# A hybrid decoder step on one core: an unsplit float32 pooling map, another order of the work up to attention, and a final norm that takes its Newton step on sums in PSUM

## The chip, the cores and the metric

The program runs on one core of a Trainium2 chip. The metric is the device time of one execution in microseconds (us). The kernel before is given by the median of three runs; one further execution was recorded by the hardware profiler, and its rows are what is quoted here.

A core has five engines that run side by side, each with its own queue of instructions, worked off in order: TensorE (PE in the profile, and PEld for its weight loads), VectorE (DVE), ScalarE (ACT), GpSimd (POOL) and SyncE (SP). An instruction that waits for another engine holds up everything behind it in its own queue. SP issues nearly all the DMAs here. POOL issues those that add what they read to what lies in SBUF.

## The reference, cut to what matters

One layer of a decoder for 1024 prompt tokens and 8 sample tokens, 1032 columns in all, width 1024:

```python
h = rmsnorm(x, g_mix); u = h @ w_in           # 512 pooling, 512 value, 512 gate columns
glu = val * sigmoid(gate)
ya = pool_mixer(a)      # windows 2/4/8/16: window mean - token; per group of 128 channels @ w_map; (+ b) * scale
yb = conv_mixer(glu)    # causal depthwise conv over 31 taps, LayerNorm over channels, silu
x = x + concat(ya, yb) @ w_out
x = x + cross_attn(rmsnorm(x, g_attn), k, v)  # 4 heads, 256 memory tokens; k, v = rmsnorm(mem) @ w_k, w_v
x = x + (silu(h @ w_gate) * (h @ w_up)) @ w_down,  h = rmsnorm(x, g_ffn)
y = x * rsqrt(mean(x * x) + 1e-6) * g_final   # the final norm
```

New keys, values and the tails of the pooling and convolution inputs are outputs too.

## The kernel before, in words

**Layout.** Channels lie on the 128 partitions and tokens along the row. A row of 1032 tokens is cut into three chunks of 344 columns for TensorE. Matrix products are made at float32 accuracy from two float32r operands each: `split` writes a rounded copy (the high half, on ACT or POOL) and the rest (the low half, on DVE or POOL), and `step3` issues three passes, high by high, high by low, low by high. `split_by_dma` makes the low half differently: ACT or POOL writes the high half and its negative, and a DMA issued by POOL adds the weights from DRAM to the negative. `BY_DMA` and `NOT_BY_DMA` say which weight tiles go that way.

**The order of the work.** Nothing is issued while the code runs: each step is a task with the engines that may do it, an estimated cost, and the buffers it reads and writes. `Program.order` then goes through the open tasks as a list scheduler: each engine takes the task that can start first by the plan, and among tasks that could start within a small slack the one with the lowest priority number. The number is the place in the program (and not above that of a follower), plus a bias. `ORDER` is the sequence, written out by hand, in which the parts up to the end of attention enter the program. A buffer is taken from a fixed number of slots of its kind: 19 large ones in SBUF (`op`), 3 for raw weights (`raw`), 2 for split weights (`w`), 3 scratch (`scr`), and in PSUM 2 wide ones of three banks (`mm`) and 2 of one bank (`ms`). So the estimated costs and the slots set the order on every queue, in later stages too. The chip then waits for semaphores, not for the plan.

**The parts that `ORDER` names and the prediction uses.** `g`, `v`, `A`: gate, value and pooling columns of `w_in`. `n`, `m`: norm and split of the memory. `K`, `V`: keys and values (tiles `kps`, `vps`, then `vf`, `vv`). `C` (`conv_sums`) and `D` (`conv_parts`): the convolution, by half-length sums (tiles `cp`, `y`) and by taps accumulated in PSUM (tile `cacc`); `s`: its sample tokens. `W` (`windows`): window sums by doubling on POOL or DVE (tile `win`), then `mean` on DVE, and a `split` of the result into `dop`, one large slot for each of the four groups. `M` (`mixer_out`): the map, `step3` on `dop` into `pmap` (a wide PSUM slot), from there ACT writes `yf` with bias and scale, and `yf` is split into `opa`. `L` (`layer_norm`): sums over channels by TensorE (`mean_ps`, `rstd_ps`), then `rsqrt_rows`, silu, split into `opb`. `O` and `B`: the output projection, first its four `opa` rows for all eight column tiles (tile `oa`), then the four `opb` rows (`ob`). After that come `q`, `S`, `T`, `P` for the prompt's attention, and `a` to `e` for the samples', which read the caches by DMA.

**After attention.** The projection `po`; then the feed-forward part as Strassen-like products of half blocks (tile `pr`), 22 tiles of gate and up, and four chunks of down; its last part, `last_down`, runs over `LAST_SPANS`, 516, 258 and 258 columns, with the rows' sums of squares collected in `fin`.

**The final norm** uses `rsqrt_rows` as the other norms do: sums over channels by a matmul with a matrix of 1/1024; on DVE m = -4(sum + eps); on ACT Ln, Exp and Square to get y = 1/(2 sqrt(sum + eps)) and y squared; on DVE t = m y^2 and y (t + 3), one Newton step, which gives 1/sqrt(sum + eps). `final` multiplies by it, for two of the eight row tiles at a time, and each pair is then written out by a DMA. `last_down` has multiplied by the weight `g_final` before.

Of the kernel before, what the change touches and what calls it, by code (L numbers as in the profile page):

```python
# [8 lines left out]
F32 = mybir.dt.float32  # L9
F32R = mybir.dt.float32r  # L10
AF = mybir.ActivationFunctionType
# [32 lines left out]
)  # L44

NOT_BY_DMA = (0, 1, 2, 16, 18, 19, 22, 23, 26, 27, 35, 36, 53, 54)
BY_DMA = ("w_in", "w_k", "w_v", "pool_map", "w_out_a", "w_out_b", "w_dn", "w_dn2")
# [5 lines left out]
SLACK = {"Pool": 0.3, "ACT": 0.3, "DVE": 0.05, "PE": 0.15}  # L53

# [15 lines left out]
    AF.Sigmoid: "sigmoid", AF.Silu: "silu", AF.Ln: "natural_log_exp_and_others", AF.Exp: "natural_log_exp_and_others",  # L70
# [18 lines left out]
class Program:  # L89
# [4 lines left out]
    SIGNAL, SIGNAL_PE, SAME = 0.2, 0.29, {"DVE": 0.12, "ACT": 0.1}  # L94

    def __init__(self, capacity):
        self.capacity = capacity
        self.tasks, self.writer, self.readers, self.later = [], {}, {}, 0

    def add(self, engines, emit, r=(), w=(), lock=False, func=None, nbytes=0):  # L100
        t = Task()
        t.engines = engines
# [140 lines left out]
def hybrid_step_kernel(ctx: ExitStack, tc: tile.TileContext, io):  # L243
# [38 lines left out]

    def act(n, ps=False, ptrs=0):
        return (0.05 if ps else 0.093) + 0.000833 * n + 0.093 * ptrs

    fixed = {"DVE": 0.065}

    def dve(n):
        return fixed["DVE"] + 0.00105 * n

    def pool_tt(n):
        return 0.09 + 0.00216 * n
# [6 lines left out]
    eps_t = const.tile([P, 1], F32, name="eps_t")  # L299
    nhalf = const.tile([P, 1], F32, name="nhalf")  # L300
# [18 lines left out]
    nc.gpsimd.memset(eps_t, EPS)  # L319
    nc.scalar.activation(nhalf, eps_t, AF.Copy)  # L320
# [42 lines left out]
    def split_by_dma(dst, key, src, n, r, again, again_keys, pool_too=False):  # L363


        def scaled(e, p, src, factor):
            if e is nc.scalar:
                e.activation(dst(p), src, AF.Copy, scale=factor)
# [6 lines left out]
        add({"Pool": 1.04}, lambda e: e.dma_start(dst(1), again(), accum_op=ALU.add), [key(1)] + again_keys, [key(1)], nbytes=4 * P * n)  # L375
# [20 lines left out]
    for part in ORDER.split():  # L396
        if part[0] == "M" and ("pool_map", 0) not in seq:
            seq.append(("pool_map", 0))
        seq += blocks.get(part[0], lambda i: [])(int(part[1:]))
# [7 lines left out]
    def w_load():  # L407
# [4 lines left out]
        width = 512 if name == "pool_map" else 1024  # L412
        raw = buf(f"raw{i}", "raw", (P, 1024))
        dma(lambda: raw[:, :width], lambda: io[name][j][:, :width], 512 * width, w=[(raw,)])
        raws[i] = (raw, width)
        state["loaded"] += 1

    def w_prep():
        i = state["prepped"]
        raw, width = raws.pop(i)  # L420
        name, j = seq[i]
        w = buf(f"w{i}", "op" if name in WIDE or i >= len(seq) - 4 else "w", (P, 2, 1024), F32R)
        if name in BY_DMA and i not in NOT_BY_DMA:
            split_by_dma(lambda p: w[:, p, :width], lambda p: (w, p), lambda: raw[:, :width], width, [(raw,)],
                         lambda: io[name][j][:, :width], [], name not in ("w_dn", "w_dn2"))
        else:
            split(lambda p: w[:, p, :width], lambda p: (w, p), lambda: raw[:, :width], width, [(raw,)])
# [23 lines left out]
    def step3(ps, w, wkeys, cols, x, k, first, last, spans=range(NCH), keys=None):  # L451
# [8 lines left out]
        add({"PE": 0.146 * 3 * len(spans)}, emit, list(wkeys) + (keys or [(x, 0), (x, 1)]),  # L460
# [12 lines left out]
    def rsqrt_rows(name, dst, dkeys, total, tkeys, ones, lo, width, at=None, more=None):  # L473
# [11 lines left out]
        for o, n in parts:  # L485
            ps = ms_buf(f"{name}_ps{o}")
            add({"PE": 0.1 + 0.0017 * n}, lambda e, ps=ps, o=o, n=n: e.matmul(
                ps[:, :n], ones, total[:, lo + o : lo + o + n], start=True, stop=more is None), tkeys, [(ps,)])
            if more is not None:
                add({"PE": 0.0017 * n}, lambda e, ps=ps, o=o, n=n: e.matmul(  # L490
                    ps[:, :n], ones, more[:, o : o + n], start=False, stop=True), [(more,)], [(ps,)])
# [16 lines left out]
    def small_products(e):  # L508
        e.tensor_tensor(pb_s, vec[:, V_PB : V_PB + 4], vec[:, V_PS : V_PS + 4], ALU.mult)
        taps = vec[:, V_CW : V_CW + 4 * CONV_K].rearrange("p (g k) -> p g k", g=4)[:, :, 1:].rearrange("p g (j two) -> p g j two", two=2)  # L510
        e.tensor_tensor(csum, taps[:, :, :, 0], taps[:, :, :, 1], ALU.add)

# [49 lines left out]
    add({"Pool": 0.5}, small_products, [("vec",)], [("small",)])  # L562
# [211 lines left out]
    a2 = [op_buf(f"a{i}") for i in range(2)]  # L774
    dops = {}

    def windows(g):
# [3 lines left out]
        tmp = op_buf(f"win{g}")  # L781
        add({"DVE": 0.07}, lambda e: e.tensor_copy(st_pool()[:, g, :, 15], ab[:, ai, SEQ:T]), [ak, (side, "pool")], [(side, "pool", g)])
# [24 lines left out]
        dops[g] = op_r(f"dop{g}")  # L807
        split(lambda p: dops[g][:, p], lambda p: (dops[g], p), cur, T, [ck])
# [11 lines left out]
    def keys(q):  # L820
        ps = mm_buf(f"kps{q}", 1)
        for i in range(2):
            w, wkeys = w_take("w_k")
            for k in range(KT):
# [4 lines left out]
                add({"PE": 0.327}, emit, wkeys + [(memg[k // 4], p, k % 4) for p in range(2)], [(ps,)])  # L829
# [62 lines left out]
    def values(c):  # L892
        ps = mm_buf(f"vps{c}", 2)
        for kk in range(4):
            w, wkeys = w_take("w_v")
            for k in (2 * kk, 2 * kk + 1):
# [6 lines left out]
                add({"PE": 1.3}, emit, wkeys + [(memg[k // 4], p, k % 4) for p in range(2)], [(ps,)])  # L903
# [76 lines left out]
    def scores(n):  # L980
# [23 lines left out]
        add({"PE": 1.31}, emit, [(qop[2 * h + dt], p) for dt in range(2) for p in range(2)] + [(kk, p, o) for p in range(2)], [pk])  # L1004
# [42 lines left out]
    def pv(n):  # L1047
# [4 lines left out]
        for c in range(2):  # L1052
# [8 lines left out]
            add({"PE": 1.3}, emit, [(v, 0), (v, 1)] + [(pT[h][m], p, c) for p in range(2) for m in range(2)], [(ps, c)])  # L1061
# [209 lines left out]
    def product(w, cols, xs, steps=1):  # L1271
# [21 lines left out]
        for n in range(0, nj, nj // steps):  # L1293
            js = range(n, n + nj // steps)
            add({"PE": 0.1195 * 6 * len(js)}, lambda e, js=js: emit(e, js),
# [230 lines left out]
    rsqrt_rows("Rf", Rf, RF, xss2, [(xss2,)], ones_d, 0, T)  # L1526
    for f in range(AHEAD):
        first_two(f)
    for f in range(FF_TILES):
# [5 lines left out]
        else:  # L1535
            fixed["DVE"] = 0.148
# [28 lines left out]

    last_w = {block: w_take(block[0]) for block in last_blocks}
# [3 lines left out]
    def last_down(c, n):  # L1570
# [19 lines left out]
        for w, keys, ks in ((wa, ka, range(4)), (wb, kb, (4, 5))):  # L1590
            add({"PE": 0.000425 * 3 * len(ks) * width}, lambda e, ks=ks: emit(e, ks),
# [8 lines left out]
        else:  # L1600
# [3 lines left out]
            e.activation(x2[j][:, i, sl], x2[j][:, i, sl], AF.Copy, scale=vcol(V_FIN, n)) if e is nc.scalar else  # L1604
            e.tensor_scalar(x2[j][:, i, sl], x2[j][:, i, sl], vcol(V_FIN, n), 1.0, ALU.mult, ALU.mult)), [xk], [xk])

    def final(c, j):
# [5 lines left out]
            [(fin, c)] + keys, keys, lock=True)  # L1613
# [126 lines left out]
```

## Time and profile before

| | |
|---|---|
| median of 3 runs | 1251.86 us (1251.17 to 1253.36) |
| profiled execution, its own time | 1254.77 us |
| its span | 1252.9 us |
| PE busy | 1215.9 us, 97% |
| DVE / ACT / POOL busy | 926.7 / 529.7 / 458.8 us |
| granted TensorE clock, mean | 0.99 |

The span is the time from the first to the last recorded event; 1.9 us of the execution's own time lie around it. A row of the timeline reads: start, duration, engine, line, operation, output and input tiles, shape, number of merged instructions, and in brackets the idle time of the engine before it with what ended that. A row of the stretches (the windows view) reads: stretch, its length, busy us and number of instructions of PE, PEld, DVE, ACT and POOL, granted TensorE clock (1.00 is full), busy share of the DMA engines, GB/s. A row of the groups (the lines view) reads: line, engine, operation, tiles, shapes, count, then busy us in all, mean ns of one, and the idle time before them.

### The profile page before, as it was taken

How to read it: one execution, taken by the hardware profiler on the slowest of the kernel's cores; microseconds unless marked ns; L12 is line 12 of the kernel's file. 1: busy time of each engine (PE TensorE's matmuls, PEld its weight loads, DVE VectorE, ACT ScalarE, POOL GpSimd, SP SyncE). 2: the span in 40 equal slices, each digit the busy share in tenths (PEclk: the TensorE clock that was granted, in tenths of full speed). 3: DMA queues.
4: the chain of work that ended last, by engine and by line, in shares of the span. 5: the costliest groups of instructions: out<-in, count | busy, mean ns of one | idle time of the engine just before them, and what ended most of it. 6: DMA issues, size and time to landing. Idle time of an engine off the chain costs nothing.

```text
span 1252.9 us, 22090 instructions
## 1 busy us (share of the span) xinstructions
PE 1215.9 (97%) x8958; PEld 1194.3 (95%) x8958; DVE 926.7 (74%) x1564; ACT 529.7 (42%) x731; POOL 458.8 (37%) x407
## 2 busy tenths in 40 slices
PE   8999996999999999999999999999999999999996
PEld 8999976999999879999999999999999999999996
DVE  7899988657367777679778677866867887778644
ACT  7766648454223453344322222222222364433644
POOL 3577841021101002113422233133324477778401
PEclk9999997999999999999999999999999999999998
DMA  7447686734255664231331332223322597778703
GB/s 281 104 84 169 142 241 177 213 88 163 104 194 207 238 225 169 102 132 38 112 126 60 111 110 102 104 67 111 106 85 89 205 312 198 206 181 206 175 26 111
DMA packets 59157, 183.86 MB, mean 147 GB/s; under 512 B 7920, under 2 KB 11696, under 8 KB 57776
## 3 DMA queue, kind: packets, MB, share of 16 engines
q1 hardware_dynamic: 52288, 157.74, 36.4%
q0 software_dynamic: 6768, 24.72, 11.2%
q8 instruction: 70, 1.15, 0.4%
q14 instruction: 31, 0.25, 0.1%
HBM read 148.80 MB, written 33.64 MB: 146 GB/s over the span
## 4 chain that ended last, share of the span: by engine, by line
PE 73%; DVE 10%; issue 7%; DMA 5%; ACT 2%; POOL 2%; SPq 0%; DVEq 0%; POOLq 0%; ACTq 0%
PE pr L1290 45%; PE ps L457 11%; PE fd L1587 6%; PE oa L457 4%; PE ob L457 4%; DVE cacc L663 2%; DMA raw<-in_w_v 2%; PE sc L1000 1%; DVE spcache_v L1097 1%; DMA spcache_k<-in_cache_k 1%; POOL w L357 1%; PE pv L1058 1%; DVE spcache_k L1097 1%; DMA w<-in_w_in 1%; DVE xss L384 1%
## 5 line engine op out<-in xcount | busy, mean ns | idle before, releaser
L1305 DVE TENSOR_TENSOR su<-pr,su 128x258 f32<-128x258 f32 (+1 forms) x204 | 109.3, 558 | 71.0 <-PE pr L1290 69.9
L1290 PE MATMUL pr<-ab,wTa 128*128 128x258 f32 x1056 | 134.2, 283 | 0.8 <-DVE su L1305 0.8
L1290 PE MATMUL pr<-ab,wG 128*128 128x258 f32 x1056 | 133.9, 283 | 0.8 <-ACT wU L346 0.8
L1290 PEld LDWEIGHTS pr<-ab,wTa 128*128 128x128 f32 x1056 | 130.1, 189 | 1.0 <-issue 1.0
L1290 PEld LDWEIGHTS pr<-ab,wG 128*128 128x128 f32 x1056 | 129.8, 189 | 1.2 <-ACT wU L346 1.1
L1290 PE MATMUL pr<-ab,wTb 128*128 128x258 f32 x1056 | 130.6, 283 | 0.0
L1290 PEld LDWEIGHTS pr<-ab,wTb 128*128 128x128 f32 x1056 | 128.6, 190 | 0.0
L457 PE MATMUL ps<-xop,w 128*128 128x344 f32 x720 | 114.1, 320 | 0.3 <-DMA w<-in_w_in 0.3
L457 PEld LDWEIGHTS ps<-xop,w 128*128 128x128 f32 x720 | 113.3, 188 | 0.6 <-DMA w<-in_w_in 0.6
L1290 PE MATMUL pr<-hb,dV 128*128 128x258 f32 x768 | 98.5, 284 | 1.1 <-ACT pp L1309 0.7
L1290 PEld LDWEIGHTS pr<-hb,dV 128*128 128x128 f32 x768 | 95.0, 189 | 1.8 <-ACT pp L1309 0.9
L457 PE MATMUL ps<-xq,w 128*128 128x344 f32 x576 | 94.8, 321 | 0.0
L457 PE MATMUL po<-oo,w 128*128 128x344 f32 x576 | 91.0, 320 | 0.4 <-DVE oo L1063 0.4
L457 PEld LDWEIGHTS po<-oo,w 128*128 128x128 f32 x576 | 90.7, 188 | 0.7 <-DVE oo L1063 0.7
L457 PEld LDWEIGHTS ps<-xq,w 128*128 128x128 f32 x576 | 90.6, 188 | 0.1
L1305 DVE TENSOR_TENSOR x<-pr,x 128x516 f32<-128x516 f32 (+1 forms) x122 | 63.3, 556 | 23.2 <-PE pr L1290 22.0
L663 DVE SCALAR_TENSOR_TENSOR cacc<-glu,vec,cacc 128x511 f32<-128x511 f32 (+14 forms) x116 | 77.0, 742 | 0.0
L1290 PE MATMUL pr<-hb,dW 128*128 128x258 f32 x576 | 75.0, 283 | 0.2 <-DVE x L1305 0.2
L1290 PEld LDWEIGHTS pr<-hb,dW 128*128 128x128 f32 x576 | 71.7, 189 | 0.4 <-DVE x L1305 0.4
L1587 PE MATMUL fd<-ho,w 128*128 128x258 f32 x576 | 70.0, 283 | 0.0
L346 ACT ACTIVATE w<-raw 128x1024 fp32r<-128x1024 f32 (+2 forms) x34 | 31.6, 932 | 90.2 <-issue 38.2
L1587 PEld LDWEIGHTS fd<-ho,w 128*128 128x128 f32 x576 | 69.5, 189 | 0.1
(323 smaller groups left out, 2338.5 us busy)
## 6 DMA issues: line engine op xcount, KB each, us to landing
gr<-in_w_gu SPq DMA_DIRECT2D x44, 512.0 KB, 3.4
hs<-hb SPq DMA_DIRECT2D x28, 516.0 KB, 4.2
hb<-su SPq DMA_DIRECT2D x8, 1032.0 KB, 4.9
dr<-in_w_dn SPq DMA_DIRECT2D x16, 512.0 KB, 6.2
hb<-hb POOLq DMA_DIRECT2D x12, 516.0 KB, 7.8
spcache_k<-in_cache_k SPq DMA_DIRECT2D x12, 512.0 KB, 5.0
raw<-in_w_in SPq DMA_DIRECT2D x10, 512.0 KB, 5.3
w<-in_w_in POOLq DMA_DIRECT2D x9, 512.0 KB, 6.6
```

The costliest lines, as they stand in the source:

```text
L346: e.activation(dst(0), src(), AF.Copy, scale=1.0 if gain is None else gain)
L357: e.tensor_tensor(dst(1), src(), f32(dst(0)), ALU.subtract)
L384: add({"Pool": pool_tt(n), "DVE": dve(n)}, lambda e: e.tensor_tensor(total(), total(), sq[:, i, :n], ALU.add), [(sq, i), tkey], [tkey], lo ...
L457: e.matmul(ps[:, c, :CW], w[:, wi, cols], x[:, xi, c * CW : (c + 1) * CW], start=first and p == 0, stop=last and p == 2)
L663: e.scalar_tensor_tensor(acc[h][:, n:], src[:, : HALF - n], w, acc[h][:, n:], ALU.mult, ALU.add)
L1000: e.matmul(bank()[:, i * NMEM : (i + 1) * NMEM], qop[2 * h + dt][:, qi, tt * P : (tt + 1) * P], kk[:, ki, 2 * (h % 2) + dt], start=(dt == ...
L1058: e.matmul(ps[:, c], v[:, vi, m, col : col + P], pT[h][m][:, pi, sl], start=(m == 0 and p == 0), stop=(m == 1 and p == 2))
L1097: e.scalar_tensor_tensor(piece[:, b], piece[:, b], 1.0, bc[:, b], ALU.mult, ALU.mult, accum_out=out(m)[:, first + b : first + b + 1])
L1290: e.matmul(bank(c), w[:, wi, cols(j)], xs[0](j, xi)[:, c * TQ : (c + 1) * TQ], start=j == 0 and p == 0, stop=j == nj - 1 and p == 2)
L1305: from_sums(sums, "DVE", dve, lambda e, src, sl: e.tensor_tensor(as_banks(o(sl), src), src, as_banks(a(sl), src), ALU.add), [akey], [okey])
L1587: e.matmul(view(i), w[:, wi, col : col + P], hops[k][:, xi, lo + i * width // count : lo + (i + 1) * width // count], start=(k == 0 and p ...
```

## The change

1. **The map.** The window results are no longer split, and `dop` is gone. `mixer_out` multiplies the raw map weights (`wmap`, one large slot, loaded when the first window part enters) with the float32 window result in one plain float32 matmul for each chunk. The map leaves the stream of split weights.
2. **The order.** A new `ORDER`, with other `LEAD`s (how far ahead a weight is prepared), a bias of 60 places on loads (0 before), and another choice of weights whose low half is made by DMA: `w_k` 1, 2, 3, 5, 7 (0 to 5 and 7 before); `w_v` 0, 1, 3, 5, 7 (0, 1, 5); `w_out_a` 0, 1, 3 (all four); `w_out_b` 2, 3 (0, 1); and now `w_q` 0, 3, 6 and `w_o` 4, 5, 6. For `w_in` and the last weights the choice stays.
3. **The planner's costs.** PE costs come from `pe(n)` and `pe32(n)`, with factors by stage in `MARGINS`; with these most costs of TensorE come out as before. A wait for TensorE's inputs is put at 0.35 us (0.29), a two-input operation on POOL at 0.05 us more, and the issue of an adding DMA on POOL at 0.6 us (1.04).
4. **The final norm.** `final_factors` takes the place of `rsqrt_rows`: ACT computes y = 1/sqrt(4 sum + 4 eps) from PSUM in one function, DVE computes (sum + eps) y from PSUM, times y, and (t - 0.75) y. The missing factor -4 is in the weights `gfin` = -4 `g_final`, made once at the start.

```diff
 ORDER = (
-    "A3 n0 g1 v1 C0 m0 g2 v2 m3 C1 m7 s0 m4 m6 g3 v3 m5 A2 A0 m1 s1 A1 m2 s2 K0 W3 K1 V1 V0 s3 W1 C2 W0 W2 K2 "
-    "M3 C3 D0 D1 M1 D2 M0 D3 K3 L0 M2 Y0 Z0 O0 O1 O2 O3 B0 B1 B2 B3 q0 q1 f0 S0 a0 b0 c0 q2 S2 q3 S4 a1 b1 S7 S6 c1 "
...
+    "m4 m7 A3 n0 g1 m0 v1 g2 v2 g3 m2 m3 m6 C0 m5 C1 m1 v3 A2 A0 s1 A1 s0 K0 s2 K1 W3 K2 V1 W0 W1 D0 s3 V0 M1 M0 "
+    "W2 C2 C3 D1 D2 M3 K3 Y0 D3 M2 L0 O0 O1 O2 O3 Z0 B0 B1 B2 B3 q0 q1 a0 f0 b0 c0 q2 q3 a1 b1 S4 S7 S0 S5 S6 c1 "
...
-LEAD = {"w_k": 4, "w_v": 3, "pool_map": 1, "w_out_a": 3, "w_q": 5, "w_in": 2, "w_out_b": 5, "w_o": 5}
+LEAD = {"w_k": 3, "w_v": 3, "w_out_a": 1, "w_q": 9, "w_in": 2, "w_out_b": 8, "w_o": 8}
-BIAS = {"evac": 10, "prep": 20, "load": 0}
+BIAS = {"evac": 10, "prep": 20, "load": 60}
...
-    SIGNAL, SIGNAL_PE, SAME = 0.2, 0.29, {"DVE": 0.12, "ACT": 0.1}
+    SIGNAL, SIGNAL_PE, SAME = 0.2, 0.35, {"DVE": 0.12, "ACT": 0.1}
...
     def windows(g):
...
+        if not dops:
+            dma(lambda: wmap[:], lambda: io["pool_map"][0], 512 * 512, w=[(wmap,)])
...
-        dops[g] = op_r(f"dop{g}")
-        split(lambda p: dops[g][:, p], lambda p: (dops[g], p), cur, T, [ck])
+        dops[g] = cur, ck
...
     def mixer_out(g):
-        if not opa:
-            state["wm"] = w_take("pool_map")
-        wmap, wmk = state["wm"]
         ps = mm_buf(f"pmap{g}")
-        step3(ps, wmap, wmk, block_cols(g), dops[g], 0, True, True)
+        cur, ck = dops[g]
+
+        def emit(e):
+            for c in range(NCH):
+                e.matmul(ps[:, c, :CW], wmap[:, block_cols(g)], cur()[:, c * CW : (c + 1) * CW], start=True, stop=True)
+
+        add({"PE": NCH * pe32(CW)}, emit, [(wmap,), ck], all3(ps))
...
+    def final_factors(c):
...
+            add({"ACT": act(n, True)}, lambda e, ps=ps, n=n, dl=dl: e.activation(
+                fin[:, dl], ps[:, :n], AF.Abs_reciprocal_sqrt, bias=eps4, scale=4.0), [(ps,), (fin, c)], [yk], func=AF.Abs_reciprocal_sqrt)
...
+            add({"DVE": dve(n)}, lambda e, ps=ps, n=n, sl=sl, dl=dl: e.scalar_tensor_tensor(
+                t[:, sl], ps[:, :n], EPS, fin[:, dl], ALU.add, ALU.mult), [(ps,), yk], [(t, sl.start)])
+            add({"DVE": dve(n)}, lambda e, sl=sl, dl=dl: e.tensor_tensor(t[:, sl], t[:, sl], fin[:, dl], ALU.mult),
+                [(t, sl.start), yk], [(t, sl.start)], lock=True)
+            add({"DVE": dve(n)}, lambda e, sl=sl, dl=dl: e.scalar_tensor_tensor(
+                fin[:, dl], t[:, sl], -0.75, fin[:, dl], ALU.add, ALU.mult), [(t, sl.start), yk], [yk], lock=True)
...
-        rsqrt_rows(f"fin{c}", fin, [(fin, c)], fin, [(fin, c)], ones_d, lo, width, more=last_sq.get(c))
+        fkeys = final_factors(c)
         for j in range(4):
-            final(c, j)
+            final(c, j, fkeys)
```

More of the change, by code (lines that the diff above doesn't have):

```diff
@@ L93 @@
     DMA_LATENCY, DMA_RATE, DMA_ISSUE, TABLE = 0.95, 0.36e6, 0.45, 1.28
-    SIGNAL, SIGNAL_PE, SAME = 0.2, 0.29, {"DVE": 0.12, "ACT": 0.1}
+    SIGNAL, SIGNAL_PE, SAME = 0.2, 0.35, {"DVE": 0.12, "ACT": 0.1}
     def __init__(self, capacity):
         self.capacity = capacity
-        self.tasks, self.writer, self.readers, self.later = [], {}, {}, 0
+        self.tasks, self.writer, self.readers, self.later, self.margin = [], {}, {}, 0, MARGINS["early"]
     def add(self, engines, emit, r=(), w=(), lock=False, func=None, nbytes=0):
         t = Task()
-        t.engines = engines
+        t.engines = {}
+        for e, cost in engines.items():
+            factor, more = self.margin.get(e, (1, 0)) if not nbytes else (1, 0)
+            t.engines[e] = cost * factor + more
         t.emit, t.lock, t.func, t.nbytes = emit, lock, func, nbytes
@@ L487, in rsqrt_rows @@
             add({"PE": 0.1 + 0.0017 * n}, lambda e, ps=ps, o=o, n=n: e.matmul(
[L488 to L491, printed above, removed]
+                ps[:, :n], ones, total[:, lo + o : lo + o + n], start=True, stop=True), tkeys, [(ps,)])
             add({"DVE": dve(n)}, lambda e, ps=ps, o=o, n=n: e.tensor_scalar(
@@ L1535, in hybrid_step_kernel @@
         else:
-            fixed["DVE"] = 0.148
+            pg.margin = MARGINS["down"]
             later(lambda: dn_load(0), "load")
@@ L1563, in hybrid_step_kernel @@
         hidden_load(f)
+    pg.margin = MARGINS["last"]
     last_w = {block: w_take(block[0]) for block in last_blocks}
```

87 lines of the change are left out of this document (57 added, 30 removed), and 4 rows, old and new, of the table ORDER.

## The prediction, made before the changed kernel was built or run

> **What bounds the kernel now.** I read the page's shares first, then the stretches of 20 us, then TensorE's own timeline where it is not full.
>
> ```profile
> PE 1215.9 (97%) x8958; PEld 1194.3 (95%) x8958; DVE 926.7 (74%) x1564; ACT 529.7 (42%) x731; POOL 458.8 (37%) x407
> ```
> ```profile
> 160.00:180.00 20.00, 20.00 (x91) 16.39 (x90) 16.14 (x26) 12.01 (x14) 7.08 (x8) 1.00 0.86 257
> 180.00:200.00 20.00, 10.77 (x70) 9.27 (x69) 19.11 (x26) 12.21 (x15) 6.00 (x7) 0.87 0.80 208
> 200.00:220.00 20.00, 16.76 (x90) 16.30 (x91) 16.61 (x20) 16.13 (x20) 3.26 (x3) 0.76 0.64 170
> 220.00:240.00 20.00, 20.00 (x116) 19.04 (x116) 15.03 (x24) 7.00 (x9) 1.94 (x2) 0.95 0.85 275
> ...
> 400.00:440.00 40.00, 37.72 (x253) 36.09 (x253) 30.02 (x106) 16.82 (x41) 3.06 (x10) 1.00 0.65 231
> 440.00:480.00 40.00, 37.46 (x215) 32.65 (x215) 34.01 (x132) 15.20 (x34) 3.88 (x12) 1.00 0.66 240
> ...
> 700.00:800.00 100.00, 100.00 (x834) 100.00 (x833) 74.05 (x107) 26.19 (x35) 32.72 (x21) 1.00 0.27 93
> ```
> TensorE is the bound: of the 1252.9 us span it is idle for 37. The stretch from 700 stands for the long middle: 834 matmuls in 100 us, no gap, so nothing to gain there. One place stands out, 180 to 220, with 12.5 us idle and the clock granted at 0.87 and 0.76. TensorE's timeline there:
>
> ```profile
> 99.79 15.74 PE L457 MATMUL ps<-xop,w 128*128 128x344 f32 x99
> ...
> 148.99 11.62 PE L827 MATMUL kps<-memg,w 128*128 128x256 f32 x96
> 160.44 22.27 PE L901 MATMUL vps<-w,memg 128*128 128x512 f32 x96
> 182.55 3.57 PE L827 MATMUL kps<-memg,w 128*128 128x256 f32 x26
> 187.98 2.86 PE L827 MATMUL kps<-memg,w 128*128 128x256 f32 x22 [1.86 <-DMA w<-in_w_k]
> 193.22 1.83 PE L457 MATMUL pmap<-dop,w 128*128 128x344 f32 x9 [2.37 <-ACT vf L906]
> 199.95 5.31 PE L457 MATMUL pmap<-dop,w 128*128 128x344 f32 x18 [4.91 <-ACT yf L848]
> ...
> 208.79 1.21 PE L457 MATMUL pmap<-dop,w 128*128 128x344 f32 x6 [0.22 <-DVE dop L357]
> ...
> 215.84 15.80 PE L457 MATMUL oa<-opa,w 128*128 128x344 f32 x81 [3.02 <-ACT yf L848]
> ```
> A 344-wide matmul takes 0.159 us when all is well (15.74/99), a 256-wide one 0.121 (11.62/96). From 182.55 to 215.84 TensorE did the last 96 `kps` and all 36 `pmap` matmuls, 11.6 + 5.7 = 17.3 us of work in 33.3 us: 16.0 lost. The five waits in brackets are 12.4 of it. The other 3.6 is clock: after the wait of 4.91 us, 18 matmuls worth 2.9 took 5.31. The first 81 `oa`, worth 12.9, took 15.8, another 2.9. So 18.9 us hang on this place.
>
> The Trainium skill, "TensorE: Matmul & The Clock Gate", Part 1, says that the array's clock is halved after an idle window of about 3.4 us and comes back only after as long a busy one. The trace agrees with it: of the waits above only the one of 4.91 us is longer than that, and the 18 matmuls right behind it run at half speed.
>
> Why TensorE starves there is read on the other engines:
>
> ```profile
> 172.89 7.86 DVE L663 SCALAR_TENSOR_TENSOR cacc<-glu,vec,cacc 128x504 f32<-128x504 f32 x12
> 176.61 0.86 POOL L375 DMA_DIRECT2D w<-in_w_k  x1 [10.58 <-ACT w L368]
> 185.75 0.68 DVE L357 TENSOR_TENSOR w<-raw,w 128x512 fp32r<-128x512 f32 x1
> 187.96 1.07 ACT L346 ACTIVATE dop<-win 128x1032 fp32r<-128x1032 f32 x1 [6.84 <-DVE win L804]
> 191.91 1.25 ACT L906 ACTIVATE vf<-vps,rmc 128x512 f32<-128x512 f32 x2
> ```
> DVE spends 7.9 us on taps while windows are still to do (`dop` waits for one until 187.96), and POOL, which may do window sums, idles 10.6. ACT then stands 6.84 us with `dop`'s high half at its head, and behind it is `vf`, which has to empty `vps`: ready at 182.7 (160.44 + 22.27), done from 191.91 on. `vps` holds one of two wide PSUM slots, and `pmap` at 193.22 had waited for `vf`.
>
> **The change, part by part.** *The map.* Four splits and one weight split go:
>
> ```profile
> L357 DVE TENSOR_TENSOR dop<-win,dop 128x1032 fp32r<-128x1032 f32 x4 | 4.9, 1230 | 2.8 <-ACT dop L346 2.8
> L346 ACT ACTIVATE dop<-win 128x1032 fp32r<-128x1032 f32 x4 | 4.2, 1055 | 6.8 <-DVE win L804 6.8
> L868 PE MATMUL mean_ps<-ysum,ones_c 128*128 128x512 f32 x4 | 1.9, 592 | 0.0
> ```
> DVE loses 4.9 + 0.7 (the weight's low half at 185.75) = 5.6 us, ACT 4.2 and its stand. Each window comes 1.06 + 1.23 = 2.3 us closer to its map. Four large slots fall away and one is added. In return TensorE multiplies in plain float32. The nearest row is `mean_ps`: two 512-wide matmuls give four records in 1.9 us, so 0.95 each, 0.64 at 344 columns; three a map, four maps: 7.7 us against 5.7, so +2.0. If cost did not fall with width it would be 12 x 0.95 = 11.4, +5.7; if the passes saved paid for all, 0. I take +2.0, as the 344- and 256-wide rows above go by width. The map's load stays one SP DMA, moved ahead of K and V loads and out of the three raw slots.
>
> *The order.* `W3 W0 W1` now stand before `V0`, `M1 M0` right behind it, ahead of `C2 C3 D1 D2 D3`; so windows may take the DVE time that taps took at 172.89, and taps move under `O`, where DVE had 5 us idle in 220 to 240 alone. If all 18.9 us go, `O` ends 18.9 - 2.0 = 16.9 earlier. But `O` covers the LayerNorm, which needs all of the convolution:
>
> ```profile
> 222.66 1.06 POOL L646 TENSOR_TENSOR y<-y,cp 128x497 f32<-128x497 f32 x1 [7.58 <-DVE y L646]
> ...
> 263.89 2.51 DVE L357 TENSOR_TENSOR opb<-y,opb 128x1032 fp32r<-128x1032 f32 x2
> 268.22 7.09 PE L457 MATMUL ob<-opb,w 128*128 128x344 f32 x44
> ```
> The convolution's last tap is at 222.66, the first `opb` is ready at 263.89 + 1.25 = 265.1, and `ob` starts at 268.22 because `O` ends there: 3.1 us of cover. So `ob` can start earlier only as far as the LayerNorm does. At worst for a gain that is 265.1 (-3.1); with DVE's 5.6 us it is 259.5 (-8.7); with `O` alone as the limit 251.3 (-16.9). I take -8.7, the one that rests on removed work and not on idle time refilled; `opb` is late next.
>
> *Weights.* `w_k` 0 and 4 and `w_out_a` 2 gain a low half on DVE or POOL, `w_v` 3 and 7 lose one: +1, at 1.23 us on DVE, and POOL's idle 10.6 us covers it; without that cover +1.2. Six `w_q` and `w_o` tiles lose theirs, and get an ACT pass (1.06) and a POOL issue (0.86) each; in 400 to 480 ACT is busy 32 of 80 us and POOL 7, so nothing, at most the six issues, +5.2, and -4.8 (both gaps of TensorE there, 2.3 + 2.5) if DVE, 64 of 80, was what it waited for. The samples' parts of `ORDER` move in the same stretch, with the same two ends. I take 0.
>
> *Planner's costs and the bias on loads.* They can reshuffle every later queue. TensorE has no gap from 600 to 1000 to close, so this can only lose. What hides it are raw weights loaded ahead:
>
> ```profile
> gr<-in_w_gu SPq DMA_DIRECT2D x44, 512.0 KB, 3.4
> ```
> One late load costs up to its 3.4 us. I take 0: loads start when one of three raw slots comes free, whatever the bias.
>
> *The final norm.* Behind the last matmul:
>
> ```profile
> 1242.85 0.70 PE L490 MATMUL fin_ps<-fsq,ones_d 128*128 128x258 f32 x2 [0.59 <-ACT fsq L1602]
> 1243.59 0.43 DVE L492 TENSOR_SCALAR fin_m<-fin_ps 128x258 f32<-128x258 f32 x1 [1.30 <-PE fin_ps L490]
> 1244.05 0.42 ACT L499 ACTIVATE fin_t<-fin_m 128x258 f32<-128x258 f32 x1 [0.71 <-DVE fin_m L492]
> ...
> 1246.33 2.52 DVE L1611 TENSOR_TENSOR x<-x,fin 128x516 f32<-128x516 f32 x4
> ```
> From 1243.59 to 1246.33 stand six steps (DVE, ACT three times, DVE twice), 0.457 each with the hop. Four remain (ACT, DVE three times): 2 x 0.457 = -0.9. The new function needs its table once, as Ln and Exp did:
>
> ```profile
> 1209.43 1.28 ACT L1636 ACT_TABLE_LOAD   x1
> ```
> It lies 33 us before the end, under `fd` matmuls. If Square were not in the new set, each change back would put 1.28 on the last span: +0.4 in sum. The first span's sums stay longer in two one-bank slots that `fd` needs too; at most one table load of waiting, +1.3. I take -0.9.
>
> Sum: -8.7 + 0 + 0 + 0 - 0.9 = -9.6 on the span of 1252.9, so 1243.3; the profiled execution took 1254.77, 2.9 above the median of 1251.86, so the median goes to 1242.3.
>
> **The rivals.**
> *Everything is recovered.* DVE's idle time fills too, and `O` is the limit: -16.9 - 0.9, so 1234. For it: POOL's long idle; against: the 42 us from the convolution's last tap to the first `opb`, which no part of the change shortens.
> *The LayerNorm stays where it is.* `ob` starts at 265.1: -3.1 - 0.9, so 1248.
> *One long wait stays.* By the two readings of the stall: if a wait as long as the 4.91 one remains, half of the 12.4 stays, and the slow clock behind it with 6.5: only -6.2 + 2.0 - 0.9, so 1247. By the rule in the Trainium skill, "TensorE: Matmul & The Clock Gate", Part 1, the slow clock is a step: a wait cut from 4.91 to 3.5 saves none of it. By a slope it would go by half too, and the sum would be 1244.
> *It doesn't do what it says.* The windows stay late for want of slots, behind K and V weights in the same large slots; -0.9 and +2.0: 1253.
> *Slower: the convolution comes last.* The windows' own work on DVE:
>
> ```profile
> L804 DVE SCALAR_TENSOR_TENSOR win<-win,a 128x1032 f32<-128x1032 f32 x4 | 4.9, 1234 | 0.1
> L791 DVE TENSOR_TENSOR win<-win 128x1022 f32<-128x1022 f32 x3 | 3.6, 1216 | 0.0
> ```
>  `C2 C3` now stand behind all windows and `V0`. If `C3`'s chain of taps, which ends at 222.66, starts later by the windows put in front (four groups, 2.4 us of last sum and mean each, so about 9), `opb` is ready at 274 and `ob` starts 6 us late: +6 - 0.9, so 1257. It decides from 4 us of delay on (3.1 of cover and 0.9 at the end). For it: 15 dependent taps in each chain; against: 5.6 us less on DVE, and an idle POOL.
>
> **How the numbers follow.** The forecast has 0.42 (1236 to 1246 by itself), everything 0.10, LayerNorm fixed 0.11, a long wait 0.12, no effect 0.09, slower 0.16. About 0.2%, 2.5 us, is what a measurement of this kernel can tell from no change. Faster is the first four, 0.75; no effect is 0.09; slower 0.16. The range goes from 1231, full recovery with most of the 4.8 us at 400 to 480 on top, to 1257.
>
> **What would show it.** Right: no `dop`; `pmap` with 24 records, about 7.7 us; TensorE's idle time in 180 to 220 under 5 us and its clock back at 1.00; `ob` starting at 255 to 262, waiting for `opb` just before; 0.9 us less between the last `fin_ps` and the first `final`. Wrong: gaps of several us in 200 to 260 behind `opb`, a granted clock under 0.9 there, waits for DMA in 320 to 480, fewer than 834 matmuls per 100 us in the middle, or a second table load after 1215.

## The result, and the profile after

The changed kernel took 1253.16 us (median of 14 runs, 1249.64 to 1259.84); the kernel before took 1251.96 us on the same chips (14 runs, 1251.17 to 1253.7). The ratio is 1.001, with a 95% interval of 1.000 to 1.0021: at most 0.2% slower and not faster. The forecast was 1242.3.

The change did most of what the sum said, and then lost it again. This table puts the two profiled executions beside each other (the changed kernel's took 1253.93 us, its span is 1252.2). Each line gives the start of a stage's first matmul on TensorE, in us.

| stage | before | after | difference |
|---|---|---|---|
| output projection, first half (`oa`) | 215.84 | 210.59 | -5.25 |
| output projection, second half (`ob`) | 268.22 | 260.33 | -7.89 |
| gate and up (`pr<-ab`) | 558.04 | 549.30 | -8.74 |
| down (`pr<-hb`) | 1006.27 | 1001.26 | -5.01 |
| last part (`fd`) | 1170.89 | 1171.11 | +0.22 |
| end of the last `fin_ps` | 1243.55 | 1243.73 | +0.18 |
| end of the span | 1252.9 | 1252.2 | -0.7 |

Up to the gate the kernel is 8.7 us ahead. The gate and up stage gives 3.7 back and the down stage 5.2. The tail behind the last `fin_ps` gains 0.9.

The early part first. TensorE's timeline of the changed kernel, to be held against that of before in the prediction:

```profile
166.72 16.82 PE L918 MATMUL vps<-w,memg 128*128 128x512 f32 x72
188.68 3.78 PE L861 MATMUL pmap<-win,wmap 128*128 128x344 f32 x6 [5.14 <-DVE win L819]
...
197.94 3.63 PE L861 MATMUL pmap<-win,wmap 128*128 128x344 f32 x12
...
207.31 1.90 PE L861 MATMUL pmap<-win,wmap 128*128 128x344 f32 x6
210.59 8.79 PE L471 MATMUL oa<-opa,w 128*128 128x344 f32 x54 [1.38 <-DVE kf L845]
...
260.33 9.90 PE L471 MATMUL ob<-opb,w 128*128 128x344 f32 x62
```

And the stretches of the same kernel (length, then busy us and count of PE, PEld, DVE, ACT and POOL, the granted clock, DMA share, GB/s):

```profile
180.00:200.00 20.00, 14.86 (x54) 10.74 (x53) 17.03 (x26) 11.47 (x13) 8.65 (x7) 0.83 0.63 174
200.00:220.00 20.00, 18.54 (x116) 16.35 (x115) 15.89 (x20) 11.48 (x14) 2.26 (x3) 1.00 0.86 234
...
600.00:1000.00 400.00, 400.00 (x3328) 400.00 (x3327) 296.89 (x423) 106.53 (x141) 127.89 (x81) 1.00 0.30 107
1000.00:1170.00 170.00, 163.96 (x1346) 162.52 (x1345) 136.02 (x216) 76.53 (x97) 130.29 (x114) 1.00 0.78 213
```

Between 180 and 220 TensorE is now idle for 6.6 us; it was 12.5. One long wait is left, 5.14 us for the window of the first map, and the clock is down behind it: six `pmap` records (two for each float32 matmul) take 3.78 us, where the last six take 1.90. Behind that all goes well, and `oa` runs at the full clock from its start. It covers the way to `ob` in 49.7 us (52.4 before), and this is 2.6 of the 7.9 us.

The middle is as full as before: 3328 matmuls in 400 us. The down stage isn't. The same stretches of the kernel before:

```profile
600.00:1000.00 400.00, 400.00 (x3330) 400.00 (x3329) 299.85 (x427) 106.58 (x143) 128.32 (x82) 1.00 0.30 104
1000.00:1170.00 170.00, 168.64 (x1391) 167.74 (x1390) 132.77 (x222) 78.78 (x98) 130.15 (x111) 1.00 0.81 221
```

From 1000 to 1170 TensorE was idle for 1.4 us, and now it is for 6.0. What it waits for from 540 to 1245 is read in the waits view (engine, what waited and for what; us in all, times, longest), first of the kernel before:

```profile
PE pr L1290 <- ACT wU L346: 0.8, 1, 0.8
PE pr L1290 <- DVE su L1305: 0.8, 1, 0.8
PE pr L1290 <- ACT pp L1309: 0.7, 1, 0.7
PE pr L1290 <- DVE x L1305: 0.6, 2, 0.4
...
```

and then of the changed one:

```profile
PE pr L1307 <- DVE x L1322: 4.0, 4, 1.8
PE pr L1307 <- ACT wG L363: 1.3, 1, 1.3
PE pr L1307 <- DVE wG L374: 1.0, 1, 1.0
PE pr L1307 <- DVE su L1322: 0.9, 1, 0.9
...
PE fd L1606 <- DVE x L1322: 0.8, 1, 0.8
...
```

`x` and `su` on DVE are the sums that empty the PSUM slots of `pr`, and `wG` is the second gate tile's weight, whose split on ACT and DVE comes late, not its load. No DMA is in the list. The tail is as forecast. ACT reads PSUM itself and DVE takes three steps:

```profile
1243.77 0.48 ACT L1642 ACTIVATE fin<-fin_ps,eps 128x258 f32<-128x258 f32 x1 [0.25 <-PE fin_ps L1640]
1244.28 0.43 DVE L1646 SCALAR_TENSOR_TENSOR fin_t<-fin_ps,fin 128x258 f32<-128x258 f32 x1 [1.81 <-ACT fin L1642]
...
1245.67 2.51 DVE L1658 TENSOR_TENSOR x<-x,fin 128x516 f32<-128x516 f32 x4
```

From 1243.77 to 1245.67 there are 1.90 us; the six steps took 2.74.

### The profile page after: what moved, and what is told of

Its sections match the earlier page's. It is cut to its first block, busy times and chain, and to the rows that moved or that the text cites. A ratio compares the mean times of both kernels' runs of the same rounds, so it can differ in the third digit from the quotient of the medians.

```text
span 1252.2 us, 22041 instructions
## 1 busy us (share of the span) xinstructions
PE 1217.0 (97%) x8946; PEld 1191.6 (95%) x8946; DVE 928.5 (74%) x1548; ACT 516.3 (41%) x715; POOL 481.8 (38%) x428
## 4 chain that ended last, share of the span: by engine, by line
PE 49%; DVE 3%; DMA 1%; issue 1%; POOL 0%; ACT 0%; DVEq 0%; SPq 0%; ACTq 0%; POOLq 0%
PE pr L1307 44%; PE fd L1606 6%; DMA dr<-in_w_dn 1%; DVE hb L374 1%; DVE x L1322 1%; DMA hs<-hb 0%; DVE dW L374 0%; POOL dt L1448 0%; DVE su L1348 0%; DVE dV L374 0%; DVE pp L1330 0%; DVE x L1658 0%; DVE pp L1322 0%; DVE dt L1448 0%; PE fin_ps L1637 0%
## 5 line engine op out<-in xcount | busy, mean ns | idle before, releaser
L1307 PE MATMUL pr<-ab,wU 128*128 128x258 f32 x528 | 67.4, 284 | 0.0
```

What stands on the lines that cost most here:

```text
L1307: e.matmul(bank(c), w[:, wi, cols(j)], xs[0](j, xi)[:, c * TQ : (c + 1) * TQ], start=j == 0 and p == 0, stop=j == nj - 1 and p == 2)
```

## The experiments

Nothing in the change touches the code of the feed-forward part. Only the planner's costs reach it, through the order on the queues. That makes the first theory: **the late costs give the early gain back.** Its rival is that a kernel that comes to the gate earlier, in another state, loses the time whatever the costs. The planner has one set of constants, so the runs change them at one point of the program, where the feed-forward part begins. Ratios are to the kernel before, on the same chip.

**e1: the old costs from the feed-forward part on.**

```diff
     pg.margin = MARGINS["gated"]
+    pg.SIGNAL_PE = 0.29
+    late["pool"] = 0.09        # pool_tt(n) returns late["pool"] + 0.00216 * n
+    issue["dma"] = 1.04        # cost of issuing an adding DMA on POOL
+    # and the bias on loads is 0 again
```

> The changed kernel, but from the feed-forward part on the planner uses the costs of before again (0.29 for TensorE's wait, 0.09 on POOL, 1.04 for an adding DMA's issue, no bias on loads). Theory A, the 7.9 us won up to `ob` and the 0.9 at the end are real and the new planner costs give the rest back by reordering the down stage: faster than before by 6 to 8.5 us, 1244 to 1246, and no wait of TensorE over 1 us between 1000 and 1180 - about 8. Theory B, the feed-forward part loses because it starts 8 us earlier, before its weights and DVE are ready, whatever the costs: no faster than the changed kernel, 1252 to 1254.

1248.52 us, ratio 0.9958 (0.9942 to 0.9973), so 5.3 us faster than before and 6.5 faster than the changed kernel by the two ratios. That is short of the 6 to 8.5 that the theory asked for. The down stage takes 165.0 us (before 164.6, changed 169.9). The rival, by which nothing would be gained over the changed kernel, falls: the same early part goes before it.

**e2: the opposite, the kernel before with the new costs from the feed-forward part on.** The same four constants, the other way round.

> The kernel before, with the new planner costs from the feed-forward part on and nothing else. Theory A: slower than before by 4 to 7 us, 1256 to 1259, with the waits for DVE behind `x` in the down stage that the changed kernel shows. Theory B: the same as before within 1 us, 1251 to 1253.

1268.22 us, ratio 1.0121 (1.0107 to 1.0135). The sign is that of the theory, the size isn't: it loses 15 us. The down stage takes 174.9, and its last wait alone is one that the changed kernel doesn't have, 5.85 us of `fd` for ACT's `w`. The late order depends on where the early part left the planner too, and what the costs do can't be taken from one kernel to another.

**e3: of the four, only the POOL constant is set back.**

```diff
     pg.margin = MARGINS["gated"]
+    late["pool"] = 0.09
```

> The changed kernel, with one planner cost alone put back from the feed-forward part on: a two-input operation on POOL at 0.09 and not 0.14 us beside its length. Theory A with POOL's cost as the one that reorders the down stage: most of what putting all back gives, 1244 to 1248. Theory A with another cost (the wait for TensorE or the issue of an adding DMA): 1252 to 1254. Theory B: 1252 to 1254.

1247.72 us, ratio 0.9958 (0.9945 to 0.9971): all of e1. 0.05 us on the planned cost of a two-input operation on POOL decide, and the other three constants do nothing in the late part that the times can tell. In the profiled executions they do move something: e3 still has the two waits for `wG` at the gate (1.11 and 0.96 us), and e1, which puts another product in between, has none. The waits of this kernel from 1000 to 1175 are

```profile
PE pr L1309 <- ACT pp L1328: 0.7, 1, 0.7
PE pr L1309 <- DVE pp L1324: 0.4, 1, 0.4
PE pr L1309 <- DVE x L1324: 0.2, 1, 0.2
```

1.3 us, where the changed kernel has 6.8 in eight waits, the first at 1001.26 and the last at 1171.11. By its median this is the fastest of all versions, though by the ratio no faster than e1, and both beat the kernel before and the changed one.

**e4: the new final norm alone, on the kernel before.**

```diff
-        rsqrt_rows(f"fin{c}", fin, ...)
+        fkeys = final_factors(c)
```

> The kernel before with the new final norm alone. By the count of steps behind the last sum (four for six, 0.457 us each): 0.9 us faster, 1251.0, in every theory. If the new function's table is loaded again between the squares: 0.4 us slower than before.

1253.16 us, ratio 0.9996 (0.9987 to 1.0004). The interval holds both nothing and -0.9 us. In the profile the way from the end of the last `fin_ps` to the end of the span is 8.64 us (9.35 before, 8.47 in the changed kernel), so the gain is there; in the time it can't be told.

**e5: the unsplit map alone, on the kernel before.**

```diff
-        split(lambda p: dops[g][:, p], ..., cur, T, [ck])
+        dops[g] = cur, ck
```

> The kernel before with the unsplit map alone: no `dop`, no split map weights, the old order, costs and choice of weights. Theory M, the map carries the gain (5.6 us less on DVE, ACT's stand gone, three large slots free): `ob` starts 5 to 8 us earlier than at 268.2 and the time falls by 4 to 8 us against before. Theory O, the new order carries it: `ob` within 2 us of 268.2 and the time within 2 us of before, with the 2.0 us of plain float32 showing. Either way `pmap` has 24 records and about 7.7 us.

1249.31 us, ratio 0.9972 (0.9963 to 0.9982): 3.5 us faster, a little less than the 4 to 8 expected of a map that carries the gain. `ob` starts at 262.73 in its profile, 5.5 us earlier than before.

**e6: the new order with the split map** (and the old late costs, so that the late loss is out of the way).

```diff
-        dops[g] = cur, ck
+        split(lambda p: dops[g][:, p], ..., cur, T, [ck])
```

> The changed kernel with the old costs from the feed-forward part on (as the first experiment) and with the split map of before in the new order. Theory M: `ob` back at 266 to 270 and the time within 1.5 us of before. Theory O: `ob` at 260 to 263 and the time 4 to 6 us below before, as in the first experiment.

1253.28 us, ratio 1.0006 (0.9998 to 1.0015): nothing. TensorE's timeline of e6 has two new long waits:

```profile
191.66 1.23 PE L479 MATMUL pmap<-dop,w 128*128 128x344 f32 x3 [5.56 <-ACT dop L368]
...
218.01 3.81 PE L479 MATMUL oa<-opa,w 128*128 128x344 f32 x12 [6.22 <-DMA w<-in_w_out_a]
```

`ob` starts at 269.08. So the order gains nothing without the unsplit map, the map alone gains 3.5 us, and the two together 5.3 (e1).

**e7: the changed kernel with all the old costs, everywhere.**

```diff
-    SIGNAL, SIGNAL_PE, SAME = 0.2, 0.35, ...
+    SIGNAL, SIGNAL_PE, SAME = 0.2, 0.29, ...
-        return 0.14 + 0.00216 * n
+        return 0.09 + 0.00216 * n
-        add({"Pool": 0.6}, lambda e: e.dma_start(...
+        add({"Pool": 1.04}, lambda e: e.dma_start(...
-BIAS = {"evac": 10, "prep": 20, "load": 60}
+BIAS = {"evac": 10, "prep": 20, "load": 0}
```

> The changed kernel with all planner costs of before in every stage, so new order, map, weights and norm under the old costs. If the costs matter only in the feed-forward part: as the first experiment, 5 us below before. If the new order needs the new costs that it was written under: pmap and `ob` later than at 191 and 262.6, and the gain falls to 0 to 3 us.

1253.28 us, ratio 1.0006 (0.9997 to 1.0015). `ob` starts at 267.09. So the new order isn't good by itself either: under the old costs it loses its gain early, and under the new ones late.

**e11: which early cost does it need?** The old late costs, and early only the POOL constant set back.

```diff
-    late = {"pool": 0.14}
+    late = {"pool": 0.09}
```

> Kernel: after, with all old costs from the feed-forward part on (0.9958 of before), and POOL's two-input cost at 0.09 also in the early part, so that of the early costs only the issue of an adding DMA (0.6), the wait for TensorE's inputs (0.35) and the load bias are new. Theory P: POOL's two-input cost decides early as well; the projection's second half starts at about 267 as with all costs old, and the ratio is about 1.000. Rival: the issue cost of the adding DMAs is what the new order needs; ob starts at 260 to 263 and the ratio is 0.995 to 0.997.

1252.52 us, ratio 0.9994 (0.9985 to 1.0002), `ob` at 266.26. It is the POOL constant again: of the two values, 0.14 gives the better time in the early part with this order, and 0.09 in the late one. The first `pmap` waits 4.83 us here for ACT's `w`, and three more waits for ACT's `yf` follow. The other early costs were not tried one by one.

**e8 and e12: two more values in the late part.** Is it that POOL is planned too slow, so that work goes to DVE and its sums come late? Then the time should rise with the constant. Or does each value only deal another order?

```diff
     pg.margin = MARGINS["gated"]
+    late["pool"] = 0.19        # e8; 0.04 in e12
```

> The changed kernel with POOL's two-input cost raised further from the feed-forward part on, to 0.19 us beside the length (0.14 in the changed kernel, 0.09 before). Theory D, a higher cost of POOL moves work to DVE, which TensorE waits for: worse than the changed kernel by 3 us or more, 5 to 9 us above before. Theory R, each cost gives another order and this one fell badly, without a direction: anywhere from 8 us below to 8 us above before, and the share of DVE in the splits of the down stage does not tell which.

> Kernel: after, with POOL's two-input cost at 0.04 from the feed-forward part on; with 0.09 (0.9958), 0.14 (1.001) and 0.19 (1.0022) the fourth point of a scan. Theory R (a cost only deals the order anew, and each order has its own gaps): no trend; anything from 0.994 to 1.003, and the down stage anywhere from 164.6 to 170. Theory D (a higher planned cost of POOL moves work onto DVE, whose sums then come later): the trend goes on, so at or below 0.9958, with the down stage at 164.6 to 165.2 and less DVE work there than the 133 us of the run with 0.09.

| late POOL constant | ratio to before (95%) | runs, us | DVE busy 1000 to 1170 | down stage |
|---|---|---|---|---|
| 0.04 (e12) | 1.0026 (1.0014 to 1.0038) | 1252.5 to 1260.0 | 132.0 | 168.8 |
| 0.09 (e3) | 0.9958 (0.9945 to 0.9971) | 1246.9 to 1249.8 | 133.3 | 165.2 |
| 0.14 (changed kernel) | 1.0010 (1.0000 to 1.0021) | 1249.6 to 1259.8 | 136.0 | 169.9 |
| 0.19 (e8) | 1.0022 (1.0009 to 1.0035) | 1252.5 to 1260.1 | 125.9 | 167.9 |

There is no trend, and the amount of DVE work doesn't explain it: the kernel with the least of it is among the slow ones. The waits of e12 from 540 to 1175 begin with

```profile
PE pr L1309 <- DVE x L1324: 3.4, 3, 1.5
PE pr L1309 <- DVE su L1324: 2.2, 3, 1.5
...
```

the same two kinds of sums, at other places. e8 loses in yet another one: its last part, from the first `fd` to the last `fin_ps`, is 4.6 us longer than the changed kernel's, with 2.6 us of waits for the DMA of `ho` and the clock at 0.50 behind them. So each constant shuffles what stands ahead of the operations that TensorE waits for. The three slow orders also spread over 7 to 10 us from run to run (12 to 14 runs each), and the fast one over 3 in its five runs; but e10 below, with the order of e3, spreads over 6 in six.

**e9 and e10: why are the sums late?** In the changed kernel the longest of these waits ends at 1043.50:

```profile
1043.50 3.15 PE L1307 MATMUL pr<-hb,dW 128*128 128x258 f32 x24 [1.80 <-DVE x L1322]
```

DVE's timeline just before it (start, duration, ...):

```profile
1037.70 5.14 DVE L374 TENSOR_TENSOR hb<-hs,hb 128x1032 fp32r<-128x1032 f32 x3
1042.76 0.68 DVE L1322 TENSOR_TENSOR x<-pr,x 128x516 f32<-128x516 f32 x1
```

and POOL's:

```profile
1038.45 1.61 POOL L1448 TENSOR_TENSOR dt<-dt,dr 128x256 f32<-128x256 f32 x1
1040.02 1.73 POOL L1448 TENSOR_TENSOR dt<-dr 128x256 f32<-128x256 f32 x1
```

Three low halves of 1032 columns (`hb`, the inputs of down) stand in front of a sum and take 1.71 us each, where the same subtraction takes 1.23 elsewhere (`dop` in the prediction). Meanwhile POOL's 256-wide differences of down weights (`dt`) take 1.6 to 1.7, where others take 0.74 and 0.75 (at 1022.47 and 1024.17). So e9 makes POOL's part cheap and leaves every queue in its order: POOL copies the first operand, and the second is left out. e10 does the same to the kernel of e3.

```diff
-            add({...}, lambda e: e.tensor_tensor(s(q)(), a(), b(), op), ...)
+            add({...}, lambda e: e.tensor_scalar(s(q)(), a(), 1.0, 1.0, ALU.mult, ALU.mult)
+                if e is nc.gpsimd else e.tensor_tensor(s(q)(), a(), b(), op), ...)
```

> Kernel: after, but where POOL makes a 256-wide difference of down weights (tile dt), it only copies the first operand; the planner still counts the same cost, so every queue keeps its order. The second operand of these differences is left out, and the output is not the reference's. Theory C (contention): in the new order of the down stage DVE's two-input operations run beside POOL's and both slow down (three hb low halves 1.71 us each beside dt at 1.6 to 1.7), and so the sums that free PSUM come late: with POOL's part cheap, TensorE's waits for DVE in 1000 to 1180 go from 6.0 us to about 2, the down stage from 169.9 to about 166, the ratio to before from 1.001 to about 0.998. Theory Q (queue order alone): the sums stand behind too much other work at any speed; the waits stay above 4 us and the ratio above 1.000.

> Kernel: the run with POOL's two-input cost at 0.09 from the feed-forward part on, with the same copies in place of differences; the same part of the computation is left out. It is the control: TensorE waits only 1.3 us for DVE and ACT in 1000 to 1170 there, so by both theories the down stage (165.2 us) goes down by at most 1 us and the ratio stays at 0.995 to 0.996. If it falls as much as the kernel with the new cost does, cheaper POOL work helps anywhere and says nothing about the order.

e9: 1251.25 us, ratio 0.9984 (0.9975 to 0.9992). e10: 1248.76 us, ratio 0.9963 (0.9949 to 0.9977), which is where e3 was. Against the changed kernel's 1.0010 that is 3.3 us less in e9, with some 1.8 of uncertainty from the two intervals, and none in the control. The same place in e9, DVE's timeline and the wait on TensorE:

```profile
1035.08 4.11 DVE L374 TENSOR_TENSOR hb<-hs,hb 128x1032 fp32r<-128x1032 f32 x3
1039.11 0.68 DVE L1322 TENSOR_TENSOR x<-pr,x 128x516 f32<-128x516 f32 x1
...
1039.85 3.17 PE L1307 MATMUL pr<-hb,dW 128*128 128x258 f32 x24 [0.77 <-DVE x L1322]
```

The three halves take 1.0 us less, and the wait of 1.80 us is 0.77. In all, from the first wait of the down stage to 1175 (it ends at 998.43 here, at 1001.26 in the changed kernel), TensorE waits 5.0 us instead of 6.8, and the down stage takes 168.4 (169.9). That is between the two theories: the ratio is what contention gave, the waits and the stage are nearer to the order alone.

And not all of the 3.3 us can be put down to the copies. In these two executions e9 is already 2.0 us shorter in the gate and up stage. Of this, 1.5 is the clock: the same 44 matmuls at the gate, some 400 us before the first copy, take 7.08 us in the changed kernel, partly at the slow clock, and 5.55 in e9 (see the last section). The copies didn't take contention away altogether, since the halves still take 1.37 each and a copy 0.68 in the mean (a difference 0.99). So: the order puts low halves in front of sums, and POOL's work beside them adds to what that costs. In the profiled executions it is 1.4 us of the 4.6 by which the changed kernel's down stage is longer than e3's; by the times it is 3.3 of 6.5, and how often the other runs met the slow clock at the gate isn't known. That it does so by slowing DVE is what the rows above show at one place; that POOL was also done sooner in e9 can't be told apart from it in the time, and how the rest is made up stays open. e3 has contention as well, with its four halves at 2.26 us each; there it falls where TensorE has work in hand, as two of them in a row cost 0.41 us of waiting.

The Trainium skill, "GPSIMD Engine Reference", 1. Specifications, says that POOL shares its SBUF interfaces with VectorE and that instructions of DVE with two SBUF inputs contend. The rows above agree with it, in both directions: 1.71 us against 1.23 on DVE, 1.6 to 1.7 against 0.75 on POOL.

## Why the prediction was wrong, step by step

**The step that failed is "Planner's costs and the bias on loads. They can reshuffle every later queue ... I take 0".** It was put at 0 with at most one late load of 3.4 us. With the old late costs back the kernel is 6.5 us faster (e1, e3), and that is what the step cost by the times. In the profiled executions 8.9 us go lost in the two stages behind the gate: 3.7 in gate and up and 5.2 in down. Of the 3.7, 2.2 are the two waits for `wG` and 1.4 the slow clock behind them, which is partly chance: of the six profiled kernels with this order at the gate four were hit (the changed one, e8, e10, e12), and e3 and e9 were not. Its sign was named ("this can only lose"), and it held late but not early, where the new cost on POOL gains 4.5 us (e1 against e11). The row that it leant on was true, TensorE had no gap from 600 to 1000 and got none. But the row covers only that stretch. From 1000 to 1170 TensorE had 1.4 us of waits in 170, with DVE at 132.8 and POOL at 130.2: two engines three quarters full whose queues served TensorE just in time. Nothing there hides another order. And the price was taken for the wrong thing: TensorE never waited for a load there. In the down stage the sums on DVE came late, and at the gate the split of a weight. No rival had the loss there; the slower one put it at the convolution.

**The map and the order, -8.7.** Measured -7.9 at `ob`, in the forecast's band of 255 to 262. But not for the reason given. DVE's timeline of the changed kernel has the first `opb` at

```profile
251.74 1.23 DVE L374 TENSOR_TENSOR opb<-y,opb 128x1032 fp32r<-128x1032 f32 x1
```

so it is ready at 253.0, the LayerNorm came 12 us earlier and not 5.6; `ob` starts at 260.33 with no wait, because `O` ends there. The limit was the first half of the projection, which regained 7.9 of the 18.9 us. The long wait for a window is left. DVE's timeline again:

```profile
173.83 4.35 DVE L819 SCALAR_TENSOR_TENSOR win<-win,a 128x1032 f32<-128x1032 f32 x1
...
181.09 5.89 DVE L675 SCALAR_TENSOR_TENSOR cacc<-glu,vec,cacc 128x501 f32<-128x501 f32 x9
...
187.19 1.23 DVE L819 SCALAR_TENSOR_TENSOR win<-win,a 128x1032 f32<-128x1032 f32 x1
```

and the last of POOL's sums for the window that is finished at 187.19:

```profile
178.18 1.89 POOL L806 TENSOR_TENSOR win<-win 128x1022 f32<-128x1022 f32 x1
```

The first window's last step runs beside POOL's window sums and takes 4.35 us instead of 1.23. And taps still stand in front of a window, as in the kernel before: POOL has done its sums by 180.07, but nine taps of 5.89 us come first in DVE's queue, and TensorE stands from 183.5 to 188.68. So the windows took the place of taps only in part, and the rival "one long wait stays" was right about the wait and about the slow clock behind it, and wrong about what it would leave of the gain.

**Plain float32 on TensorE, +2.0.** 24 records, as forecast; 18 of them at the full clock take 5.53 us, so all would take 7.4 against 5.7: +1.7.

**The weights, 0.** From `ob` to the gate the changed kernel gains another 0.85 us. Right within its ends.

**The final norm, -0.9.** -0.88 in the changed kernel, -0.71 alone. One table load lies at 1209.70, as forecast.

**The reading that only the wait of 4.91 us is long enough for the slow clock.** It was wrong. The 81 `oa` matmuls behind the wait of 3.02 us, which the prediction itself found slow, ran at a granted clock of 0.50 at first (last section). No term of the sum rests on it, but the rival of the one long wait does.

The sum as measured on the spans is -7.89 - 0.85 + 3.73 + 5.23 - 0.04 (last part) - 0.88 = -0.7. Without the failed step it would be -9.7, nearly the forecast's own sum, and this is luck: two of its terms were each off by less than a microsecond in opposite directions. Over several runs less of it is left: e3, with the old late order, is 5.3 us faster and not 9.6. In the profile of e1, where no wait for `wG` is left, the same sum is -5.6 - 1.0 + 0.7 + 0.4 + 0.0 - 0.7 = -6.2: there the map and the order give 3.1 us less than the forecast had. For e3, `ob` starts at 262.43 with the same early order as the changed kernel's 260.33, so a single execution is good to some 2 us there, and the gate still waits 2.1 us for `wG`.

## What to carry to other kernels

When a planner sets the order of every queue, a change of one cost is a change of every stage that comes behind it; price it at the stage whose second and third engines are nearly full, not at the one where TensorE has no gap. Let a new constant hold only where it was found to be good: here 0.05 us on one operation was worth 4.5 us early (e1 against e11) and cost 6.5 us late, with no trend from one value to the next. Before trusting an order, look at what stands in front of the operations that empty PSUM, and at what the neighbouring engine runs at that time.

## What the runs showed of the hardware

**The slow clock doesn't need one long wait.** The prediction named only the wait of 4.91 us as long enough. But the stretches of the kernel before, behind the wait of 3.02 us that ends at 215.84, read

```profile
216.00:218.00 2.00, 2.00 (x8) 2.00 (x9) 1.89 (x4) 2.00 (x4) 0.00 (x0) 0.50 1.00 204
...
222.00:224.00 2.00, 2.00 (x14) 2.00 (x14) 1.08 (x2) 0.00 (x0) 1.06 (x1) 1.00 1.07 422
```

Half the clock, with 8 matmuls in 2 us instead of 14. Shorter waits can do it too. The changed kernel waits 1.28 and 0.96 us at the gate, with 0.75 us of matmuls between:

```profile
558.44 0.75 PE L1307 MATMUL pr<-ab,wG 128*128 128x258 f32 x4 [1.28 <-ACT wG L363]
560.15 4.06 PE L1307 MATMUL pr<-ab,wG 128*128 128x258 f32 x21 [0.96 <-DVE wG L374]
```

Its stretch behind that, and then the same place in e3, which waits 1.11 and 0.96 us:

```profile
562.00:564.00 2.00, 2.00 (x11) 2.00 (x10) 2.00 (x5) 1.34 (x3) 0.00 (x0) 0.50 0.00 0
```

```profile
562.00:564.00 2.00, 2.00 (x17) 2.00 (x18) 2.00 (x4) 1.89 (x4) 0.00 (x0) 1.00 0.04 8
```

Nearly the same waits, the slow clock in one kernel and not in the other; it cost the changed kernel another 1.4 us (21 matmuls in 4.06 us, worth 2.64 at the 0.126 of the 42 ahead of them). It isn't the order either: e10, with the order of e3, was hit there (44 matmuls in 7.08 us), and e9, with the changed kernel's, wasn't (5.55).

The traces' record of the clock shows what is common to these places. In each of the 14 executions all changes of the clock lie a whole number of steps of 3.413 us apart. It falls 27 times before TensorE's work is done, each time at the end of such a step, and in that step TensorE had been idle for 1.59 us or more in sum. Of the steps at full clock without a fall, none had more than 1.89. (The ends of matmuls are modelled, so both are rough.) So about half a step of idle time was enough here, in however many waits, and whether a pair of short waits falls into one step is chance.

The Trainium skill, "TensorE: Matmul & The Clock Gate", Part 1, says that the window of about 3.4 us is free-running and doesn't start anew with the kernel. The steps agree with it, and so does a place that is hit in one execution and missed in another; that a window must be idle as a whole doesn't, as the falls above show.

**Two-input operations on DVE and POOL slow each other.** 1.23 us became 1.71 to 4.35 on DVE, and 0.75 became 1.6 to 1.7 on POOL, in the rows above.

**The same order doesn't run alike each time.** An order with TensorE waiting for DVE's sums spread over 7 to 10 us from run to run (the table of the four constants), but e10, with hardly any such wait, over 6.3 in six runs, so these waits alone don't explain it. In the seven kernels with one early order (the changed one, e1, e3, e8, e9, e10, e12) `ob` started between 259.31 and 262.89. The kernel before spread over 5.7 us in 35 runs.
